# A two-layer hybrid trunk: eight heads' rows of the first output projection in full float32, and another order of its rows

## The chip, the cores and the metric

The program runs on one core of a Trainium2 chip. The time is the device time of one execution in microseconds; the kernel before is timed in three runs, and their median is used. The engines of the core work side by side, each through its own list of instructions in order: TensorE (PE in the profile, its loads of stationary operands PEld), VectorE (DVE), ScalarE (ACT), GpSimd (POOL) and SyncE (SP), which here only issues transfers.

## The reference, cut to what matters

A decoder of two layers over 256 positions of width 2048, in float32. Layer 0 mixes with a forgetting attention of 16 heads, layer 1 with a windowed attention; after each mixer comes a gated ConvFFN. A conditioning vector c gives shift, scale and gate of every sub-layer.

```python
for i in range(DEPTH):
    mod = c_act @ ada_w[i] + ada_b[i]
    sh1, sc1, g1, sh2, sc2, g2 = jnp.split(mod[:, None, :], 6, axis=-1)
    h = x * (1.0 + sc1) + sh1
    y = fox_attention(...) if i % 2 == 0 else swa_attention(...)
    x = layer_norm(DEEPNORM_ALPHA * x + (1.0 + g1) * y, ...)
    h = x * (1.0 + sc2) + sh2
    y = conv_ffn(...)
    x = layer_norm(DEEPNORM_ALPHA * x + (1.0 + g2) * y, ...)
...
def fox_attention(h, w_in, b_f, w_o):
    ...
    o = o.transpose(1, 0, 2, 3, 4).reshape(B, S, FOX_WIDTH)
    return o @ w_o
```

The place of the change is the last line: the outputs of the 16 heads, 256 x 2048, times w_o, 2048 x 2048. One head is 128 columns of o and 128 rows of w_o.

## The kernel before, in words

Large products are made in fp32r, a rounded form of float32. To keep float32's accuracy each operand is split into a high half (the rounded value) and a low half (what is left), and three products are made for one: high with high, high with low, low with high. Of the weights, `stream` (L231) loads a raw tile w, four row blocks of 128 by 512 columns (1 MB), ScalarE casts two row blocks to wh (L252), and VectorE takes the difference wl (L264). Of the heads, ScalarE casts the output o from PSUM (L84) and VectorE takes the difference (L85), into tiles oT or, for heads 12 to 15, into the store hH of the layer's input, which is no longer needed.

The output projection (`out_proj`, L765) multiplies with the heads as the stationary operand and 512 columns of weights moving. There are four column blocks d and eight pairs of heads kc in each. One pair in one column block is a unit: two halves of the sequence, two heads, three products, 12 in all. Column blocks 0 and 1 are done side by side in three stretches of rows, 0 to 7, 8 to 11 and 12 to 15; then block 2 and block 3 run through all rows. In block 3 the last four units do the first half of the sequence first, so that its LayerNorm can start (`x_mm_end`, `Edge.end`).

The heads are begun in blocks of four in the order 0, 2, 1, 3 (heads 0 to 3, 8 to 11, 4 to 7, 12 to 15) and run as generators behind the matrix products: each unit ends with `tick`, which moves every running head by a step: scores S, softmax (pr, with its sums on VectorE at L721 and L733 and its exponentials on ScalarE at L725 and L735), transposes T with their copy pT, and the product with V, o. If a unit needs a head that is not ready, `stat` steps the heads until it is. The same `tick` advances the conditioning: 0.72 columns a unit, each a 1 MB transfer wa and a reduction on VectorE (L406).

The raw tiles w, the columns wa and the rows of the LayerNorm share one pool of six buffers of 1 MB, and SyncE issues their transfers in program order, each when its buffer is free. A scheduler merges all this into one list for each engine, which then runs in that order.

Of the kernel before, what the change touches and what calls it, by code (L numbers as in the profile page):

```python
# [17 lines left out]
P = 128  # L18
# [23 lines left out]
def hybrid_trunk(ctx: ExitStack, tc: tile.TileContext, a: dict, out: bass.AP):  # L42
# [34 lines left out]
    def pin(ins, on=True):  # L77

        if on:
            tc.keep_in_program_order(ins)  # L80
# [145 lines left out]

    halves = []

    def stream(wsrc, row0, col, ks, use, spare={}):

        ks, pend = list(ks), {}  # L231
        for kc in ks[::2]:
            g = row0 + kc
            src = wsrc[g // UK, col // WB]
            if kc in pend:
                w = pend[kc]
            elif g % UK == 0 and kc + 2 in ks:
                W = wtile()
                pin(nc.sync.dma_start(W, src), False)
                w, pend[kc + 2] = W[:, :2], W[:, 2:]  # L240
            else:
                if halves:
                    w = halves.pop()
                else:
                    W = wtile()
                    w = W[:, :2]
                    halves.append(W[:, 2:])
                pin(nc.sync.dma_start(w, src[:, g % UK:g % UK + 2]), False)
            h, l = spare[kc]() if kc in spare else (hl.tile([P, 2, WB], F32R, tag=n, name=n) for n in ("wh", "wl"))
            pieces = [(h, l, w)] if not isinstance(h, Pair) else [(h[:, i, :], l[:, i, :], w[:, i, :]) for i in range(2)]  # L250
            for hp, _, wp_ in pieces:
                pin(nc.scalar.copy(hp, wp_), False)  # L252

            def go(kc=kc, h=h, l=l):
                ahead[0] -= 1
                run_post()
                use(kc, h, l)
                if feeds:
                    feeds.pop(0)()
                tick()  # L260

            def residual_(pieces=pieces, go=go):
                for hp, lp, wp_ in pieces:
                    nc.vector.tensor_tensor(lp, wp_, f32(hp), op=ALU.subtract)  # L264
# [126 lines left out]
    def tick():  # L391
        ada_tick()
        if not feeds:
            side_step()
            step()
# [360 lines left out]

    AV = ((0, 0, 2 * P), (P, 2 * P, 3 * P))

    def o_tile(kc):

        if kc >= KC - 4:
            return hH[:, kc, :], hL[:, kc, :]
        g = gtile("oT")
        return g[:, 0, :], g[:, 1, :]

    def out_proj(oT, full, w_o, l, edge):
        def stat(kc, t):
            while kc not in full:
                step()
            return oT[kc][0][:, t * P:(t + 1) * P], oT[kc][1][:, t * P:(t + 1) * P]  # L770

        ps = {d: x_banks() for d in range(2)}

        def part(d, ks):
            if d == D // WB - 1:
                stream(w_o, 0, d * WB, ks, x_mm_end(ps[d], stat, KC, HEAD, edge.end), spares(KC, HEAD, True))
            else:
                stream(w_o, 0, d * WB, ks, lambda kc, h, l_: x_mm(ps[d], kc, h, l_, stat, KC - 1))

        for i, ks in enumerate((range(0, 8), range(8, 12))):  # L780
            then(lambda i=i: ada.update(rate=(0.72, 0.43)[l]))
            for d in range(2):
                part(d, list(ks))
        then(lambda: (ada_need(l, 2), ada.update(rate=(0.72, 0.65)[l])))
        for d in range(D // WB):
            if d < 2:
                part(d, list(range(12, KC)))
            else:
                ps[d] = x_banks()
                part(d, list(range(KC)))  # L790
            if d < D // WB - 1:
                then(lambda d=d: defer(residual(ps[d], d, gates[l, 2], True)))
                then(lambda d=d: ada.update(rate=(0.72, 0.65)[l] if d < D // WB - 2 else 0.0))
        then(lambda: (flush(), ada.update(gate_free=True)))


    def fox(l, j, edge):
# [84 lines left out]
        def head(blk, hh, q, k, V):  # L882
# [22 lines left out]
            def outputs(pT):  # L905
                ops = bank("o")
                for b, (d0, s0, s1) in enumerate(AV):
                    mm(ops[:, d0:S], V[b][:, hs], pT[:, s0:s1], start=b == 0, stop=b == 1, skip_group_check=True)
                oT[h] = o_tile(h)
                full.add(h)  # L910
                split(*oT[h], ops[:, :S])

            hs = slice(hh * P, (hh + 1) * P)
            yield from attend(scores, outputs)
# [94 lines left out]
    def swa(l, j, edge, after):  # L1009
# [49 lines left out]
        def pair(g, n, q):  # L1059
# [39 lines left out]
            oT[kc] = o_tile(kc)  # L1099
            full.add(kc)  # L1100
            split(*oT[kc], ops[:, :S])

        ps = head_block(w_in, KOFF, after.start)
        then(lambda: ada.update(rate=.1))
# [163 lines left out]
```

## Time and profile before

| | us |
|---|---|
| median of three runs (2185.02 to 2186.53) | 2186.52 |
| profiled execution | 2185.4 |
| its span, first to last instruction | 2183.6 |
| output projection of layer 0, first product to the first turn of x behind it | 337.3 to 456.3 |

Mean granted clock of TensorE 0.994. A row of the timeline gives start, duration, engine, line, operation, the tile written and the tiles read, the shape, how many instructions are merged into the row, and in brackets the idle time of the engine ahead of it with what ended it. A row of groups gives total busy time, the mean of one in ns, and the idle time before them. TensorE's rows overlap: one product's end is covered by the next one's start, so the pace is read from starts.

### The profile page before, as it was taken

Reading aid. Unit: us, or ns where it says so; the run is one execution under the profiler, and the core shown is the slowest. Engines: PE = TensorE matmul, PEld = TensorE weight load, DVE = VectorE, ACT = ScalarE, POOL = GpSimd, SP = SyncE. Lnnn points to the kernel's source line nnn. Section 1 sums busy time; section 2 is a strip of 40 time slices with the busy share of each in tenths; the row PEclk is TensorE's granted clock in tenths of the full one; section 3 lists DMA queues with packets and bytes.
Section 4 is the critical chain, followed back from the end, with each engine's and each line's share of the span. In section 5 each row is a group of like instructions: output and inputs, shape, how many; then the busy total and the mean of one; then the engine's idle time right before and its main releaser. Section 6 shows DMA issues by size and latency. Waiting matters only on the chain.

```text
span 2183.6 us, 35813 instructions
## 1 busy us (share of the span) xinstructions
PE 2129.5 (98%) x14488; PEld 1932.3 (88%) x14488; DVE 1763.2 (81%) x2425; ACT 1169.7 (54%) x1805; POOL 11.8 (1%) x34
## 2 busy tenths in 40 slices
PE   6999999899999999999999999999999999999997
PEld 6999887779999888999987877779999888999986
DVE  7988899989889988898997897779788655666765
ACT  4546566445575433555555677655555633555541
POOL 1000000000000000000000000000000000000000
PEclk9999999999999999999999999999999999999999
DMA  9998988948888999887885665547777555555552
GB/s 387 421 372 302 369 332 339 348 171 337 315 301 315 336 344 362 324 329 293 326 327 231 250 251 193 172 146 297 272 270 272 199 194 195 195 195 195 193 195 99
DMA packets 89654, 598.60 MB, mean 274 GB/s; under 512 B 10016, under 2 KB 12352, under 8 KB 21136
## 3 DMA queue, kind: packets, MB, share of 16 engines
q1 hardware_dynamic: 89312, 595.87, 73.7%
q8 instruction: 113, 1.85, 0.3%
q0 software_dynamic: 176, 0.44, 0.1%
q14 instruction: 53, 0.43, 0.1%
HBM read 594.18 MB, written 2.10 MB: 273 GB/s over the span
## 4 chain that ended last, share of the span: by engine, by line
PE 82%; DVE 10%; ACT 5%; issue 1%; DMA 1%; SPq 0%; POOL 0%; DVEq 0%; ACTq 0%; POOLq 0%
PE ws L75 46%; PE xs L75 34%; DVE wa L406 3%; DVE wl L264 3%; ACT wh L252 2%; DMA w<-in_fox_w_in_dram 1%; ACT pr L725 1%; DVE pr L721 1%; PE o L75 0%; DVE x L646 0%; ACT pr L1088 0%; DVE stats L648 0%; PE T L752 0%; PE sm L75 0%; PE sm L488 0%
## 5 line engine op out<-in xcount | busy, mean ns | idle before, releaser
L252 ACT CAST wh<-w 128x1024 fp32r<-128x1024 f32 x712 | 749.1, 1055 | 748.0 <-PE xs L75 336.5
L264 DVE TENSOR_TENSOR wl<-w,wh 128x1024 fp32r<-128x1024 f32 x712 | 866.4, 1223 | 328.5 <-ACT wh L252 325.9
L75 PE MATMUL ws<-hH,wh 128*128 128x256 f32 x6400 | 1098.0, 276 | 8.0 <-ACT hH L515 7.2
L75 PEld LDWEIGHTS ws<-hH,wh 128*128 128x128 f32 x6400 | 968.3, 188 | 11.4 <-ACT hH L515 7.6
L75 PE MATMUL ws<-hH,wl 128*128 128x256 f32 x3200 | 879.9, 276 | 2.4 <-DVE wl L264 2.4
L75 PEld LDWEIGHTS ws<-hH,wl 128*128 128x128 f32 x3200 | 601.3, 188 | 3.4 <-DVE wl L264 3.4
L406 DVE CUSTOM_DVE_ANT_0 wa<-wa,cb,acol 128x2048 f32<-128x2048 f32 x192 | 450.0, 2347 | 0.2 <-DVE cb L134 0.2
L75 PE MATMUL xs<-wh,gT 128*128 128x512 f32 x1344 | 414.7, 389 | 0.0
L75 PEld LDWEIGHTS xs<-wh,gT 128*128 128x128 f32 x1344 | 252.3, 188 | 52.1
L75 PE MATMUL xs<-wh,hH 128*128 128x512 f32 x800 | 269.4, 402 | 6.2 <-ACT wh L252 2.4
L75 PE MATMUL xs<-wl,gT 128*128 128x512 f32 x672 | 261.4, 389 | 0.0
L75 PEld LDWEIGHTS xs<-wh,hH 128*128 128x128 f32 x800 | 149.3, 189 | 41.8 <-ACT hH L84 3.5
L75 PE MATMUL xs<-wl,hH 128*128 128x512 f32 x400 | 158.4, 396 | 3.3 <-DVE wl L264 3.3
L75 PEld LDWEIGHTS xs<-wl,gT 128*128 128x128 f32 x672 | 126.1, 188 | 26.3
L1123 ACT ACTIVATE u<-ws,ccol 128x256 f32<-128x256 f32 x176 | 97.0, 563 | 51.8 <-PE ws L75 42.1
L75 PE MATMUL xs<-wh,oT 128*128 128x512 f32 x352 | 119.1, 407 | 0.2 <-ACT oT L84 0.2
L1124 DVE SCALAR_TENSOR_TENSOR u<-ws,ccol,u 128x255 f32<-128x255 f32 x176 | 82.6, 479 | 14.0 <-ACT u L1123 14.0
L75 PEld LDWEIGHTS xs<-wl,hH 128*128 128x128 f32 x400 | 75.6, 189 | 18.6 <-DVE wl L264 3.9
L1126 DVE SCALAR_TENSOR_TENSOR u<-ws,ccol,u 128x254 f32<-128x254 f32 x176 | 83.8, 480 | 2.2
L75 PEld LDWEIGHTS xs<-wh,oT 128*128 128x128 f32 x352 | 68.2, 194 | 15.6 <-ACT oT L84 0.7
L75 PE MATMUL xs<-wl,oT 128*128 128x512 f32 x176 | 71.2, 405 | 6.8 <-DVE wl L264 6.8
L725 ACT ACTIVATE pr<-pr,nm 128x128 f32<-128x128 f32 x96 | 43.3, 454 | 29.9 <-DVE nm L721 29.7
(210 smaller groups left out, 1195.2 us busy)
## 6 DMA issues: line engine op xcount, KB each, us to landing
wa<-in_ada_w_dram SPq DMA_DIRECT2D x192, 1024.0 KB, 6.9
w<-in_ffn_w_up_dram SPq DMA_DIRECT2D x176, 1024.0 KB, 5.1
w<-in_ffn_w_down_dram SPq DMA_DIRECT2D x88, 1024.0 KB, 5.0
w<-in_fox_w_in_dram SPq DMA_DIRECT2D x60, 512.0 KB, 8.3
w<-in_swa_w_in_dram SPq DMA_DIRECT2D x20, 1024.0 KB, 5.6
w<-in_fox_w_in_dram SPq DMA_DIRECT2D x18, 1024.0 KB, 7.4
w<-in_fox_w_o_dram SPq DMA_DIRECT2D x16, 1024.0 KB, 6.9
w<-in_swa_w_o_dram SPq DMA_DIRECT2D x16, 1024.0 KB, 4.8
```

Source lines behind the costliest of these rows:

```text
L75: return nc.tensor.matmul(o, lhsT, rhs, start=start, stop=stop, **kw)
L252: pin(nc.scalar.copy(hp, wp_), False)
L264: nc.vector.tensor_tensor(lp, wp_, f32(hp), op=ALU.subtract)
L406: return nc.vector.tensor_tensor_reduce(w, w, cb, 1.0, acol[:, l, v * KC + k:v * KC + k + 1], ALU.mult, ALU.add, cv[:, k:k + 1])
L721: nc.vector.tensor_tensor_reduce(pr[:, b:e].rearrange("p (a k) -> p a k", k=P), S_ps[:, b:e].rearrange("p (a k) -> p a k", k=P), mk, -1.0, ...
L725: nc.scalar.activation(pr[:, b:e], pr[:, b:e], AF.Exp, bias=nm[:, r:r + 1], scale=-1.0, accum_out=ss[:, r:r + 1])
L1123: nc.scalar.activation(u, pf, AF.Identity, bias=cw(CW, f), scale=cw(2, f))
L1124: nc.vector.scalar_tensor_tensor(u[:, 1:], pf[:, :S - 1], cw(1, f), u[:, 1:], op0=ALU.mult, op1=ALU.add)
L1126: nc.vector.scalar_tensor_tensor(u[:, 2:], pf[:, :S - 2], cw(0, f), u[:, 2:], op0=ALU.mult, op1=ALU.add)
```

## The change

In layer 0, heads 4 to 7 and 12 to 15 are whole: ScalarE copies their output unrounded to a float32 tile oW (two heads to a tile), and nothing is left over for a low half. The rows of w_o that belong to them are not cast and have no residual: the raw tile w is the moving operand, and there is one float32 product where there were three. Of the 32 units of the projection 16 are whole: four of the eight pairs in each of the four column blocks. In column blocks 0 and 1 the rows come in the order 0 to 3, 8 to 11, 4 to 7, 12 to 15. The second layer's projection is as before.

```diff
-    def stream(wsrc, row0, col, ks, use, spare={}):
+    def stream(wsrc, row0, col, ks, use, spare={}, whole=()):
...
+            if kc in whole:
+                add(kc, w, None, use)
+                continue
             h, l = spare[kc]() if kc in spare else (hl.tile([P, 2, WB], F32R, tag=n, name=n) for n in ("wh", "wl"))
...
-            def residual_(pieces=pieces, go=go):
+            def split_(pieces=pieces):
                 for hp, lp, wp_ in pieces:
                     nc.vector.tensor_tensor(lp, wp_, f32(hp), op=ALU.subtract)
-                del residuals[go]
-
-            ahead[0] += 1
-            weights.add(go)
+
+            add(kc, h, l, use, split_)
+
+    def add(kc, h, l, use, split_=None):
+
+        def go():
+            ahead[0] -= 1
+            run_post()
+            use(kc, h, l)
+            if feeds:
+                feeds.pop(0)()
+            tick()
+
+        def residual_():
+            split_()
+            del residuals[go]
+
+        ahead[0] += 1
+        weights.add(go)
+        if split_:
             residuals[go] = residual_
-            work.append(go)
-            settle(2)
+        work.append(go)
+        settle(2)
 
     def x_mm(ps, kc, h, l, stat, last, first=0, ts=range(NT), js=range(2)):
 
         for t in ts:
             for i in js:
                 xh, xl = stat(kc + i, t)
+                if l is None:
+                    mm(ps[t], xh, h[:, i, :], start=kc + i == first, stop=kc + i == last)
+                    continue
                 mm(ps[t], xh, h[:, i, :], start=kc + i == first)
                 mm(ps[t], xh, l[:, i, :])
                 mm(ps[t], xl, h[:, i, :], stop=kc + i == last)
...
-    def o_tile(kc):
-
+    WHOLE = ((*range(4, 8), *range(12, KC)), ())
+
+    wide = []
+
+    def o_tile(kc, src, l):
+
+        if kc in WHOLE[l]:
+            if not wide:
+                g = f32(gtile("oW"))
+                wide.extend(g[:, i, :] for i in range(2))
+            o = wide.pop(0)
+            nc.scalar.copy(o, src)
+            return o, None
         if kc >= KC - 4:
-            return hH[:, kc, :], hL[:, kc, :]
-        g = gtile("oT")
-        return g[:, 0, :], g[:, 1, :]
+            o = hH[:, kc, :], hL[:, kc, :]
+        else:
+            g = gtile("oT")
+            o = g[:, 0, :], g[:, 1, :]
+        split(*o, src)
+        return o
...
-        for i, ks in enumerate((range(0, 8), range(8, 12))):
-            then(lambda i=i: ada.update(rate=(0.72, 0.43)[l]))
+        early, late = (range(0, 8), range(8, 12)) if l else ((*range(0, 4), *range(8, 12)), range(4, 8))
+        for ks in (early, late):
+            then(lambda: ada.update(rate=(0.72, 0.43)[l]))
             for d in range(2):
                 part(d, list(ks))
```

The lists of three engines show what moves. First TensorE, at the third stretch of rows, where the heads of block 3 end. Before, a unit with the transposes T of one of them ahead of the next unit:

```order
L752 MATMUL T<-ident,pr 128x128 x3
L75 MATMUL xs<-wh,oT 128x512
L75 MATMUL xs<-wl,oT 128x512
L75 MATMUL xs<-wh,oT 128x512 x2
L75 MATMUL xs<-wl,oT 128x512
L75 MATMUL xs<-wh,oT 128x512 x2
L75 MATMUL xs<-wl,oT 128x512
L75 MATMUL xs<-wh,oT 128x512 x2
L75 MATMUL xs<-wl,oT 128x512
L75 MATMUL xs<-wh,oT 128x512
L752 MATMUL T<-ident,pr 128x128 x3
```

Now:

```order
L75 MATMUL xs<-w,oW 128x512 x4
L766 MATMUL T<-ident,pr 128x128 x3
L75 MATMUL xs<-w,oW 128x512 x4
L766 MATMUL T<-ident,pr 128x128 x3
L75 MATMUL xs<-w,oW 128x512 x4
L75 MATMUL o<-pT,v 128x256
L75 MATMUL o<-pT,v 128x128
L766 MATMUL T<-ident,pr 128x128 x3
L75 MATMUL xs<-w,oW 128x512 x4
L75 MATMUL o<-pT,v 128x256
L75 MATMUL o<-pT,v 128x128
```

A unit of 12 products has become one of four, and the ends of the heads stand closer together, one or two whole units ahead of the rows that need them.

Second VectorE, ahead of the residuals for the fifth and sixth unit of column block 2 (t, x and stats are the LayerNorm rows of the finished column blocks 0 and 1; ISA rows are the reductions wa, each with the read of its sum). Before:

```order
L644 TENSOR_TENSOR t<-xs,gate 128x512
L648 BN_STATS stats<-x 128x6
L406 ISA wa,cv<-wa,cb,acol 128x2048
L406 ISA cv 128x1
L264 TENSOR_TENSOR wl<-w,wh 128x1024
L646 TENSOR_TENSOR x<-x,t 128x512
L264 TENSOR_TENSOR wl<-w,wh 128x1024
L648 BN_STATS stats<-x 128x6
L406 ISA wa,cv<-wa,cb,acol 128x2048
L406 ISA cv 128x1
L644 TENSOR_TENSOR t<-xs,gate 128x512
L646 TENSOR_TENSOR x<-x,t 128x512
```

These are followed by stats, one more wa and the two residuals. Now:

```order
L658 TENSOR_TENSOR t<-xs,gate 128x512 x2
L660 TENSOR_TENSOR x<-x,t 128x512 x2
L662 BN_STATS stats<-x 128x6
L420 ISA wa,cv<-wa,cb,acol 128x2048
L420 ISA cv 128x1
L662 BN_STATS stats<-x 128x6
L420 ISA wa,cv<-wa,cb,acol 128x2048
L420 ISA cv 128x1
L259 TENSOR_TENSOR wl<-w,wh 128x1024 x2
```

The residuals of the third and fourth unit, which stood among these rows, are gone; the LayerNorm rows and the columns wa have stayed.

Third SyncE's list of transfers with what each waits for, at the same place in both programs (DVE, PE and Activation are the engines whose last read frees the buffer, DMAHW an earlier transfer). Before:

```order
L405 DMA wa<-in_ada_w_dram 128x2048 [waits DMAHW2_49,DVE_49]
L239 DMA w<-in_fox_w_o_dram 128x2048 [waits DMAHW4_49,DMAHW3_49,DVE_49]
L405 DMA wa<-in_ada_w_dram 128x2048 [waits DVE_49]
L405 DMA wa<-in_ada_w_dram 128x2048 [waits DMAHW6_49,DMAHW5_49,DVE_49]
L239 DMA w<-in_fox_w_o_dram 128x2048 [waits DVE_49]
L405 DMA wa<-in_ada_w_dram 128x2048 [waits DMAHW7_49,DMAHW1_49,DVE_49]
L239 DMA w<-in_fox_w_o_dram 128x2048 [waits DMAHW0_49,DVE_49]
```

Now:

```order
L419 DMA wa<-in_ada_w_dram 128x2048 [waits DMAHW2_49,DVE_49]
L239 DMA w<-in_fox_w_o_dram 128x2048 [waits DMAHW3_49,DVE_49]
L419 DMA wa<-in_ada_w_dram 128x2048 [waits DMAHW4_49,PE_49]
L419 DMA wa<-in_ada_w_dram 128x2048 [waits DMAHW5_49,DVE_49]
L239 DMA w<-in_fox_w_o_dram 128x2048 [waits DMAHW6_49,DVE_49]
L419 DMA wa<-in_ada_w_dram 128x2048 [waits DMAHW7_49,PE_49]
L239 DMA w<-in_fox_w_o_dram 128x2048 [waits DMAHW0_49,DVE_49]
```

The sequence of the transfers is the same; two of the columns wa shown, and five in the projection, now wait for TensorE, since a raw tile of whole rows is read by TensorE itself.

More of the change, by code (lines that the diff above doesn't have):

```diff
@@ L775, in part @@
             if d == D // WB - 1:
-                stream(w_o, 0, d * WB, ks, x_mm_end(ps[d], stat, KC, HEAD, edge.end), spares(KC, HEAD, True))
+                stream(w_o, 0, d * WB, ks, x_mm_end(ps[d], stat, KC, HEAD, edge.end), spares(KC, HEAD, True), WHOLE[l])
             else:
-                stream(w_o, 0, d * WB, ks, lambda kc, h, l_: x_mm(ps[d], kc, h, l_, stat, KC - 1))
-        for i, ks in enumerate((range(0, 8), range(8, 12))):
-            then(lambda i=i: ada.update(rate=(0.72, 0.43)[l]))
+                stream(w_o, 0, d * WB, ks, lambda kc, h, l_: x_mm(ps[d], kc, h, l_, stat, KC - 1), whole=WHOLE[l])
+        early, late = (range(0, 8), range(8, 12)) if l else ((*range(0, 4), *range(8, 12)), range(4, 8))
+        for ks in (early, late):
+            then(lambda: ada.update(rate=(0.72, 0.43)[l]))
             for d in range(2):
```

15 lines of the change are left out of this document (3 added, 12 removed).

## The prediction

> **What bounds the kernel now.** First the page's top, then the output projection by stage (length, then busy time of TensorE, its weight loads, VectorE, ScalarE and GpSimd, granted clock, share of the DMA engines, GB/s).
>
> ```profile
> span 2183.6 us, 35813 instructions
> PE 2129.5 (98%) x14488; PEld 1932.3 (88%) x14488; DVE 1763.2 (81%) x2425; ACT 1169.7 (54%) x1805; POOL 11.8 (1%) x34
> ...
> 337.30:355.10 17.80, 13.40 (x57) 10.33 (x57) 15.23 (x27) 13.12 (x32) 0.00 (x0) 0.90 0.85 321
> 355.10:400.20 45.10, 45.10 (x225) 37.71 (x224) 42.65 (x64) 24.26 (x48) 0.00 (x0) 1.00 0.92 342
> 400.20:426.60 26.40, 23.86 (x97) 19.06 (x96) 23.10 (x24) 8.42 (x8) 0.00 (x0) 0.94 0.92 354
> 426.60:456.30 29.70, 25.02 (x97) 19.30 (x95) 23.87 (x32) 9.04 (x10) 0.57 (x1) 0.89 0.73 273
> sum 119.00, PE 107.38 PEld 86.39 DVE 104.85 ACT 54.84 POOL 0.57; mean PE 26.84 PEld 21.60 DVE 26.21 ACT 13.71 POOL 0.14
> ```
>
> The kernel as a whole is TensorE's; these 119.0 us are not. TensorE is idle for 119.0 - 107.38 = 11.6 us of them, and where it had been idle the granted clock falls to 0.90, 0.94 and 0.89. The timeline of TensorE shows the waits, the waits in this stretch the engine behind them:
>
> ```profile
> 338.28 0.33 PE L752 MATMUL T<-ident,pr 128*128 128x128 f32 x1 [0.86 <-ACT pr L735]
> ...
> 348.77 0.84 PE L752 MATMUL T<-ident,pr 128*128 128x128 f32 x3 [3.23 <-ACT pr L735]
> 414.29 0.50 PE L75 MATMUL xs<-wl,oT 128*128 128x512 f32 x1 [2.54 <-DVE wl L264]
> 437.27 0.80 PE L75 MATMUL xs<-wl,oT 128*128 128x512 f32 x1 [4.25 <-DVE wl L264]
> ...
> PE xs L75 <- DVE wl L264: 6.8, 2, 4.3
> ```
>
> Two waits are for wl, the low half of a weight pair, from VectorE; the 3.23 are for a head of block 1 (heads 4 to 7), asked for while it is still in its softmax. For the price of TensorE's work I read the chain of waits where TensorE ran without a gap (start, length, what):
>
> ```profile
> 364.14 0.92 PE S L75 x8
> 368.73 2.75 PE xs L75 x12
> 371.48 0.33 PE T L752 x3
> 377.67 0.65 PE o L75 x4
> ```
>
> A unit (two heads' rows of the weights against both halves of the sequence, 12 products) takes 2.75 us; of a head, the scores S take 0.92, the transposes T 0.33, the product with V (o) 0.65. The stretch holds 32 units, 4 S, 8 T and 8 o: 88.0 + 3.7 + 2.6 + 5.2 = 99.5 us. **Lost: 119.0 - 99.5 = 19.5 us**, idle and slow clock together. The 57 records up to 355.1 are 36 products (3 units), 12 of T, 8 of o and one at the edge, 10.9 us: 6.9 lost. In the last two stages (56.1 us, 16 units, 44.0 us) 12.1 are lost, in the second 0.5.
>
> **The change part by part.** *TensorE.* 16 of the 32 units become whole: four products of full float32 for twelve of fp32r. The trace has full float32 in o; two products of a head, 256 and 128 columns, are four records. By shape:
>
> ```profile
> L75 PE MATMUL ws<-hH,wh 128*128 128x256 f32 x6400 | 1098.0, 276 | 8.0 <-ACT hH L515 7.2 <-DVE hH L517 0.8
> L75 PE MATMUL o<-pT,v 128*128 128x256 f32 x32 | 9.5, 379 | 0.0
> ```
>
> 32 records for 16 heads: each such product is two records. Each lasts 103 ns longer than an fp32r record of the same shape, some 230 columns more at the unit's 2.75 us / (12 x 512) = 0.448 ns a column: it reads its columns about twice. So a full product is four passes, and one for three is more work, not less. Pace: 0.65 us for 2 x (256 + 128) = 768 record columns, 0.846 ns; a 512-column record 0.433, a product 0.867, a whole unit 3.47 us. **Added: 16 x (3.47 - 2.75) = 11.5 us**, on the engine that sets the pace. Bounds: four unoverlapped halves of 379 ns a product, 1.52 us, give 6.1 us a unit and +53 us; two records at fp32r pace, 0.46, give 1.8 and -15 us. I take the o pace, the same kind of operand in a stream, and allow 0.79 to 0.90 ns a column (3.24 to 3.67 a unit): the one from eight records of o in a row (1536 columns, 1.22 us to the next start), the other two fp32r passes of 0.448.
>
> ```profile
> 355.11 1.47 PE L75 MATMUL o<-pT,v 128*128 128x256 f32 x8
> 356.33 0.30 PE L75 MATMUL S<-Bm,A 128*128 128x128 f32 x1
> ```
>
> [...]
>
> *VectorE and ScalarE.* Groups of the 119.0 us:
>
> ```profile
> L406 DVE CUSTOM_DVE_ANT_0 wa<-wa,cb,acol 128x2048 f32<-128x2048 f32 x18 | 42.2, 2342 | 0.0
> L264 DVE TENSOR_TENSOR wl<-w,wh 128x1024 fp32r<-128x1024 f32 x32 | 38.6, 1220 | 4.1 <-ACT wh L252 4.0
> L648 DVE BATCH_NORM_STATS2 stats<-x 128x6 f32<-128x512 f32 x7 | 4.8, 689 | 0.0
> L644 DVE TENSOR_TENSOR t<-xs,gate 128x512 f32<-128x512 f32 x7 | 4.8, 688 | 8.7 <-PE xs L75 8.7
> L646 DVE TENSOR_TENSOR x<-x,t 128x512 f32<-128x512 f32 x7 | 4.8, 685 | 0.0
> ...
> 410.76 2.33 DVE L406 CUSTOM_DVE_ANT_0 wa<-wa,cb,acol 128x2048 f32<-128x2048 f32 x1
> 413.02 0.08 DVE L406 DVE_READ_ACCUMULATOR2_ANT cv<- 128x1 f32 x1
> 413.02 2.36 DVE L264 TENSOR_TENSOR wl<-w,wh 128x1024 fp32r<-128x1024 f32 x2
> ```
>
> Two wl in a row take 2.36 us, a wa 2.26. VectorE loses 16 wl (18.9 us) and 8 low halves of oT; ScalarE 16 casts. This alone is worth nothing; it pays where VectorE makes TensorE wait. In the last two stages VectorE works 23.10 + 23.87 = 47.0 us against TensorE's 44.0, and the loads of the later units stand behind conditioning columns (wa) and LayerNorm rows. After, it is 47.0 - 8 x 1.18 = 37.6 against 8 x 2.75 + 8 x 3.47 = 49.8.
>
> Does the order allow it? At the first of the two waits, column block 2 begins at 400.2 and its fifth unit got wl at 414.29, 14.1 later. Now VectorE has, from the start of the block, two t, two x, two stats (0.69 each), two wa (2.26) and one wl (1.18) ahead of that unit: 9.8 us. TensorE asks after two split and two whole units, 12.4 us. At the second, two t, a wa, two x, two stats and one product for G and B precede the first remaining residual: some 8 us, asked for after 12.4. **Both waits go: -12.1 us.**
>
> *Heads.* The first eight units are now rows 0 to 3 and 8 to 11, whose heads are done; block 1 has until about 370 (355.1, four more units, four S and one o). But the first units stand behind the same work:
>
> ```profile
> 342.57 2.35 DVE L406 CUSTOM_DVE_ANT_0 wa<-wa,cb,acol 128x2048 f32<-128x2048 f32 x1
> 345.57 1.03 ACT L252 CAST wh<-w 128x1024 fp32r<-128x1024 f32 x1
> 346.63 1.23 DVE L264 TENSOR_TENSOR wl<-w,wh 128x1024 fp32r<-128x1024 f32 x1 [0.55 <-ACT wh L252]
> 348.32 0.80 ACT L735 ACTIVATE pr<-pr,ss 128x128 f32<-128x128 f32 x2
> ```
>
> TensorE stands from 345.5 to 346.6 for wh, then 0.7 for wl, then 0.3 for pr, after the 0.9 before its first T; with an estimated 0.6 at the restarts 3.6 are lost instead of 6.9, **-3.3 us**. [...] New: where a head's o is copied just ahead of its use, TensorE waits for that copy:
>
> ```profile
> 389.53 0.37 ACT L84 CAST hH<-o 128x256 fp32r<-128x256 f32 x1
> ```
>
> Heads 12 and 13, then 14 and 15: 0.37 and the latency, 0.55 twice, **+1.1**.
>
> *Transfers.* Their number and bytes stay; what changes is how long a raw weight tile is held: until TensorE's last read, no longer until VectorE's. Six buffers serve the weights and wa, and five wa issues now wait for TensorE. Landing times of the projection's loads, and the queue's longest wait for VectorE before:
>
> ```profile
> DMA to landing us min/median/max: 4.8/6.9/8.9
> ...
> SPq L239 <- DVE wl L264: 31.3, 9, 8.2
> ```
>
> A held tile is freed at the end of its second unit. Behind the issue that waits for it stand the loads of later units, and the tightest is that for units five and six of column block 2. Bound: if the tile waited for is the one read last before that block, the load is third behind it: 6.9, twice 3.0 (1.05 MB at 354 GB/s), cast 1.05 and wl 1.18, 15.1 us against 12.4, so 2.7 late. If it is any earlier whole tile, the load has at least 6.9 us more and nothing is late. The other buffers turn over faster than the held ones, so an older tile is likelier: **0**, the bound kept for a rival.
>
> **Sum:** 11.5 - 12.1 - 3.3 + 1.1 = **-2.8 us**. The profiled execution took 2185.4 us, 1.8 outside its span, and lies 1.1 below the median of 2186.5; 2.8 off gives 2182.6 for it and **2183.7** for the median. The gain is what is left of 15.4 us of waits after 12.6 us of price.
>
> **The rivals.** (1) *Larger gain.* Full float32 runs at 0.79 ns a column and a whole unit takes 3.24 us: 3.7 less, 2180.0; if VectorE's shorter queue also clears half of the early wait, 2178.2. For it: eight records in a row ran so, and no stream of 512-column full products is in the trace. Against: the four of a head, the commoner case, took 0.846. (2) *No change.* A pass costs what an fp32r pass costs, a whole unit 3.67: +3.2, 2186.9. For it: xs runs at 0.448 ns a column where o runs at 0.423 a pass, so streams of 512 columns may be the slower ones. Against: o has weight loads of the same size and more switches. [...] (3) *Slower: held tiles starve the fifth unit.* Place: units five and six of column blocks 2 and 3. Price: 2.7 us each by the bound above, and after each a slow clock, which in the last two stages came to 12.1 - 2.54 - 4.25 = 5.3 us for two waits, so 2.7 + 2.7 twice, 10.8: 2194.5; in one block alone 2189.1. It decides from the point where wl comes more than 12.4 us after the block began. For it: DMA was at 0.92 of its time in both stages, and the queue issues in order. Against: TensorE is the slower engine there by 49.8 to 37.6, and an earlier tile leaves 6.9 us. (4) That the change does not do what it says is ruled out by the program's order: the whole units are there, the residuals gone.
>
> **How the numbers follow.** Chances: forecast 0.50, larger gain 0.22, no change 0.14, slower 0.14. 0.2% is 4.4 us, about what a measurement of this kernel can tell from no change, so the forecast itself lies within it. It spreads by the pace (0.79 to 0.90 ns, 3.7 down and 3.2 up) and by a microsecond or two of heads: of its 0.50, 0.13 are faster by more than that, 0.36 within and 0.01 slower. The larger gain is faster with all of its 0.22; of no change 0.13 are within and 0.01 faster; of slower 0.12 are slower and 0.02 within. Together **faster 0.36, same 0.51, slower 0.13**. The range runs from rival 1's lower end to a little past one starved block: **2178 to 2190.5**.
>
> **What would show it.** Right: xs from w and oW with 128 records (16 units x 4 products x 2), starting 0.43 us apart, a whole unit in 3.47; no wait of TensorE for wl over 1 us in the two last column blocks, granted clock near 1.00 there; about 3.5 us lost before the ninth unit, and waits of some 0.5 us for the copy of o; 16 wl fewer; the stage about 116 us instead of 119.0, and the stages behind it unchanged. Wrong: a record pace away from 0.433 moves the time by 1.28 us for each 0.01; a wait for wl or for a w transfer at a fifth unit is rival 3; a stage that shortens with a total that does not means that the gain is given back in the ConvFFN behind it.

## The result, and the profile after

| | before | after |
|---|---|---|
| median on the same chip, 10 runs each | 2186.11 | 2180.15 |
| profiled execution | 2185.4 | 2180.0 |
| its span | 2183.6 | 2178.1 |
| first product of the stage to the ConvFFN's first turn of x | 131.8 | 126.7 |

The ratio is 0.9978, with a 95% interval of 0.9970 to 0.9986: faster by 6.0 us by the medians, by 4.8 us (3.1 to 6.6) by the ratio. The forecast was 2183.7, a gain of 2.8 us, within a range of 2178 to 2190.5; by the medians the change gained twice that. The prediction thought it likeliest that the gain stays within 0.2%; the interval has that bound inside it. Of all executions in this document three took 3401, 4320 and 4351 us (one of vector_back, one of the kernel before, one of four_split); the ratios leave them out, and without them the medians of vector_back and four_split below are 2179.98 and 2183.79.

The last row of the table is a length that all kernels below have too. Its ends are these two rows of TensorE's timeline, first before, then after:

```profile
338.37 0.72 PE L75 MATMUL xs<-wh,oT 128*128 128x512 f32 x2
...
470.20 0.65 PE L488 MATMUL sm<-ident,x 128*128 128x128 f32 x4
```

```profile
337.98 0.72 PE L75 MATMUL xs<-wh,oT 128*128 128x512 f32 x2
...
464.68 0.66 PE L502 MATMUL sm<-ident,x 128*128 128x128 f32 x4
```

5.1 of the 5.5 us that the span lost are in this stage. The page's first line and the stage by windows, after (length, then busy time of TensorE, its weight loads, VectorE, ScalarE and GpSimd, granted clock, share of the DMA engines, GB/s):

```profile
span 2178.1 us, 35629 instructions
...
336.90:354.80 17.90, 15.43 (x74) 12.04 (x74) 14.97 (x25) 13.97 (x33) 0.00 (x0) 1.00 0.84 313
354.80:401.10 46.30, 46.30 (x178) 28.90 (x176) 33.25 (x50) 14.22 (x38) 0.00 (x0) 1.00 0.90 335
401.10:425.70 24.60, 24.60 (x81) 15.03 (x80) 21.00 (x23) 4.01 (x4) 0.00 (x0) 1.00 0.97 378
425.70:450.80 25.10, 24.51 (x80) 14.70 (x78) 15.38 (x23) 5.99 (x6) 0.57 (x1) 1.00 0.76 284
sum 113.90, PE 110.84 PEld 70.67 DVE 84.61 ACT 38.19 POOL 0.57; mean PE 27.71 PEld 17.67 DVE 21.15 ACT 9.55 POOL 0.14
```

TensorE is busier than before in the stage (110.84 against 107.38), yet the stage is 5.1 us shorter. The granted clock is 1.00 in all four windows, where it was 0.90, 0.94 and 0.89 in three. The new operation, by its tile oW, and TensorE's timeline at the places of which the prediction spoke:

```profile
L75 PE MATMUL xs<-w,oW x128: 590/592/667, 370.0 to 452.2; 128*128 128x512 f32 x128
L784 ACT COPY oW<-o x8: 350/372/373, 349.5 to 391.3; 128x256 f32<-128x256 f32 x8
```

```profile
346.27 0.73 PE L75 MATMUL xs<-wh,oT 128*128 128x512 f32 x2 [1.09 <-ACT wh L255]
347.53 0.50 PE L75 MATMUL xs<-wl,oT 128*128 128x512 f32 x1 [0.53 <-DVE wl L259]
...
370.00 3.60 PE L75 MATMUL xs<-w,oW 128*128 128x512 f32 x8
373.43 0.49 PE L766 MATMUL T<-ident,pr 128*128 128x128 f32 x3
...
406.96 7.03 PE L75 MATMUL xs<-w,oW 128*128 128x512 f32 x16
414.06 0.40 PE L75 MATMUL xs<-wl,oT 128*128 128x512 f32 x1
...
450.83 1.11 PE L539 MATMUL sm<-ident,x 128*128 128x128 f32 x8 [0.63 <-DVE x L688]
```

A whole unit, eight records, takes 373.43 - 370.00 = 3.43 us (3.44 over 17 units in a row, in whole_all below). Between 347.5 and 450.2 TensorE waits for nothing: the waits of 2.54 and 4.25 us are gone. By the prediction's count the work in the stage is now 16 x 2.75 + 16 x 3.44 + 11.5 for the heads = 110.5 us, so 113.9 - 110.5 = 3.4 us are lost, where 19.5 were.

### The profile page after: what moved, and what is told of

Same layout as the page of the kernel before. It is cut to its first block, busy times and chain, and to the rows that moved or that the text cites. A ratio compares the mean times of both kernels' runs of the same rounds, so it can differ in the third digit from the quotient of the medians.

```text
span 2178.1 us, 35629 instructions
## 1 busy us (share of the span) xinstructions
PE 2133.7 (98%) x14424; PEld 1916.9 (88%) x14424; DVE 1742.4 (80%) x2400; ACT 1151.8 (53%) x1788; POOL 11.8 (1%) x34
## 4 chain that ended last, share of the span: by engine, by line
PE 84%; DVE 9%; ACT 4%; DMA 2%; issue 1%; SPq 0%; POOL 0%; DVEq 0%; ACTq 0%; POOLq 0%
PE ws L75 46%; PE xs L75 35%; DVE wa L420 3%; DVE wl L259 2%; DMA w<-in_fox_w_in_dram 2%; ACT wh L255 1%; DVE pr L735 1%; PE o L75 1%; PE S L75 1%; ACT pr L739 0%; PE T L766 0%; ACT hH L551 0%; PE sm L75 0%; PE sm L502 0%; DVE hH L552 0%
## 5 line engine op out<-in xcount | busy, mean ns | idle before, releaser
L255 ACT CAST wh<-w 128x1024 fp32r<-128x1024 f32 x698 | 733.0, 1053 | 726.8 <-PE ws L75 340.2
L259 DVE TENSOR_TENSOR wl<-w,wh 128x1024 fp32r<-128x1024 f32 x698 | 847.8, 1221 | 328.6 <-ACT wh L255 326.1
L75 PE MATMUL xs<-wh,hH 128*128 128x512 f32 x752 | 254.0, 403 | 6.5 <-ACT wh L255 3.2
L75 PEld LDWEIGHTS xs<-wh,hH 128*128 128x128 f32 x752 | 140.3, 189 | 40.3 <-ACT wh L255 3.7
L75 PE MATMUL xs<-wl,hH 128*128 128x512 f32 x376 | 148.9, 396 | 2.5 <-DVE wl L259 2.5
L75 PE MATMUL xs<-wh,oT 128*128 128x512 f32 x288 | 96.1, 401 | 1.1 <-ACT wh L255 1.1
L75 PEld LDWEIGHTS xs<-wl,hH 128*128 128x128 f32 x376 | 71.0, 189 | 16.9 <-DVE wl L259 3.2
L75 PEld LDWEIGHTS xs<-wh,oT 128*128 128x128 f32 x288 | 53.9, 188 | 13.2 <-ACT wh L255 1.3
L658 DVE TENSOR_TENSOR t<-xs,gate 128x512 f32<-128x512 f32 x48 | 31.5, 683 | 35.0 <-PE xs L75 35.0
```

The lines of the kernel that those rows point to most:

```text
L75: return nc.tensor.matmul(o, lhsT, rhs, start=start, stop=stop, **kw)
L658: pin(nc.vector.tensor_tensor(tmp, ps[t], gate[:, d * 512:(d + 1) * 512], op=ALU.mult), end)
```

## The experiments

All times are medians of 5 to 11 runs; each kernel was timed together with the kernel before, whose medians on those chips were 2184.4 to 2185.3. "Stage" is the length defined above, from each kernel's profiled execution; in the last two kernels the work ahead of the first product lies otherwise, and the length is left out.

| kernel | time | ratio to before, 95% | stage |
|---|---|---|---|
| before | 2186.11 | | 131.8 |
| the change | 2180.15 | 0.9978 (0.9970 to 0.9986) | 126.7 |
| order_only | 2184.01 | 0.9996 (0.9987 to 1.0005) | 131.1 |
| whole_old_order | 2179.87 | 0.9978 (0.9970 to 0.9987) | 126.6 |
| whole_4to7 | 2177.05 | 0.9965 (0.9952 to 0.9977) | 124.0 |
| whole_12to15 | 2183.60 | 0.9996 (0.9987 to 1.0005) | 130.8 |
| vector_back | 2180.16 | 0.9978 (0.9968 to 0.9987) | 126.7 |
| from_vector | 2180.73 | 0.9981 (0.9972 to 0.9990) | 126.6 |
| four_split | 2183.86 | 0.9995 (0.9986 to 1.0004) | 129.9 |
| from_copy | 2179.92 | 0.9977 (0.9968 to 0.9986) | 126.8 |
| late_4to7 | 2178.21 | 0.9968 (0.9956 to 0.9980) | 124.8 |
| whole_all | 2184.95 | 0.9999 (0.9990 to 1.0007) | 133.6 |
| first_units | 2178.36 | 0.9971 (0.9960 to 0.9982) | |
| first_late | 2177.37 | 0.9968 (0.9956 to 0.9980) | |

### The two edits apart

*order_only*: nothing whole, rows in the new order.

```diff
-    WHOLE = ((*range(4, 8), *range(12, KC)), ())
+    WHOLE = ((), ())
```

> The new order of the rows (0 to 3, 8 to 11, 4 to 7, 12 to 15) with no whole rows: three products and all splits stay. Theory (two separate effects: the order clears the early wait for heads 4 to 7, the whole rows clear the two waits for wl in column blocks 2 and 3 and cost TensorE 11.0 us): the early part gains about 3.5 us, the two late waits stay, and a part of the early gain is lost there since VectorE sets the time from 394 us on: 2182.5 to 2185. Rival (the order is the whole gain and the float32 products only cost): faster than the full change, 2175 or less.

2184.01 us, within the theory's range, and no difference from the kernel before that can be told. Its timeline shows the early part cleared as in the change, and the late waits back, the first of them longer than the 2.54 of before:

```profile
346.26 0.73 PE L75 MATMUL xs<-wh,oT 128*128 128x512 f32 x2 [1.09 <-ACT wh L255]
...
412.87 0.80 PE L75 MATMUL xs<-wl,oT 128*128 128x512 f32 x1 [4.32 <-DVE wl L259]
...
436.75 0.50 PE L75 MATMUL xs<-wl,oT 128*128 128x512 f32 x1 [3.75 <-DVE wl L259]
```

Most of what the order gains early, TensorE spends in longer waits for wl: 9.3 us in blocks 2 and 3 (0.46 and 0.78 beside the two shown), where it was 6.8.

*whole_old_order*: the eight heads whole, rows 0 to 7, then 8 to 11.

```diff
-        early, late = (range(0, 8), range(8, 12)) if l else ((*range(0, 4), *range(8, 12)), range(4, 8))
+        early, late = range(0, 8), range(8, 12)
```

> Heads 4 to 7 and 12 to 15 whole as in the change, rows in the old order (0 to 7, 8 to 11). Theory: TensorE pays 11.0 us, the two late waits (12.1 us with their slow clock) go, the wait for heads 4 to 7 at 345 us stays: 2184 to 2187. Rival (the order is the whole gain): 2186.1 + 11.0, about 2197. Rival (the whole rows are the whole gain): 2180.

The rival held: the same time as the change. One early wait is left, for the copy of a head of block 1, half of the 3.23 us of before, and none up to the LayerNorm:

```profile
348.20 1.13 PE L75 MATMUL xs<-w,oW 128*128 128x512 f32 x2 [1.68 <-ACT oW L784]
```

So the order is worth nothing that can be told here, alone or beside whole rows.

### Which rows

*whole_4to7* and *whole_12to15*: only one half of the whole heads, new order.

```diff
-    WHOLE = ((*range(4, 8), *range(12, KC)), ())
+    WHOLE = ((*range(4, 8),), ())
```

```diff
-    WHOLE = ((*range(4, 8), *range(12, KC)), ())
+    WHOLE = ((*range(12, KC),), ())
```

> Only heads 4 to 7 whole, heads 12 to 15 split as before the change; the new order. Theory: the price on TensorE is half, 5.5 us; both late waits still go, since in column block 2 the fifth unit asks for its low half 12.3 us after the block began and VectorE has 9.8 us ahead of it, and in column block 3 the unit that waited 4.25 us is one of the whole ones: 2186.1 - 3.5 - 12.1 + 5.5, about 2176. Rival (relief goes by the number of whole units): midway between the order alone and the full change, 2181 to 2183.

> Only heads 12 to 15 whole, heads 4 to 7 split; the new order. Theory (it counts where in a column block the low halves are missing, not how many): the price is 5.5 us, but in column block 2 the fifth unit asks after 11.0 us with 12.2 us of VectorE's work ahead of it, a wait of 1 us or more, and the third unit of column block 3 waits as before, 4 us with a slow clock behind it: 2182 to 2185. Rival (any half of the whole rows does): as with heads 4 to 7, about 2176.

Both times came as expected. Heads 4 to 7 alone, half the price, lie 3.1 us below the change (the stage is 2.7 us shorter, though the intervals of the two ratios overlap) and have one late wait, at the first unit of block 3; heads 12 to 15 alone leave both. First the timeline of the former, then of the latter:

```profile
425.05 0.50 PE L75 MATMUL xs<-wl,oT 128*128 128x512 f32 x1 [1.45 <-DVE wl L259]
```

```profile
413.92 0.50 PE L75 MATMUL xs<-wl,oT 128*128 128x512 f32 x1 [2.41 <-DVE wl L259]
436.25 0.50 PE L75 MATMUL xs<-wl,oT 128*128 128x512 f32 x1 [4.25 <-DVE wl L259]
```

The first wait is at the fifth unit of block 2, the second at the third unit of block 3. Heads 4 to 7 are the third and fourth units of a block: just ahead of the first wait, and at the place of the second itself. Heads 12 to 15 are the seventh and eighth: behind the first wait, and two units ahead of the second.

### VectorE's relief, or TensorE's pace

The prediction laid the late waits to VectorE's load. A whole unit spares VectorE a residual, waits for nothing that VectorE makes, and keeps TensorE 0.69 us longer. Three kernels part these.

*vector_back*: VectorE gets its work back, and nobody reads it.

```diff
             if kc in whole:
-                add(kc, w, None, use)
+                idle = hl.tile([P, 2, WB], F32R, tag="wl", name="wl")
+                def idle_(w=w, idle=idle):
+                    nc.vector.tensor_tensor(idle, w, w, op=ALU.subtract)
+                add(kc, w, None, use, idle_)
```

> The change, and for each of its 16 whole units VectorE also runs an operation of the shape of a residual, whose result nothing reads (wl = w - w, 128x1024): the work of VectorE is that of before again, the work of TensorE that of the change. Theory: VectorE is relieved by 1.2 us a unit, but a whole unit needs no result of VectorE at all, and TensorE asks for the fifth unit of a column block later by 0.69 us for each whole unit ahead of it; of the 12.1 us of late waits at most some 2 to 4 come back, as waits for wl of 1 to 2 us at the first split unit behind the whole ones. 2181 to 2184 us. Rival: it is the shorter queue of VectorE alone that clears them; then both waits return with 2.5 us or more each, and with the price of 11.0 us still paid the time is 2189 or more. Second rival: the queue is worth nothing, 2180.

2180.16 us, the time of the change: the second rival. VectorE's groups and the timelines of VectorE and TensorE at the fifth unit of block 2:

```profile
L253 DVE TENSOR_TENSOR wl<-w 128x1024 fp32r<-128x1024 f32 x16 | 19.1, 1213 | 0.0
```

```profile
412.04 2.36 DVE L264 TENSOR_TENSOR wl<-w,wh 128x1024 fp32r<-128x1024 f32 x2
```

```profile
413.84 0.40 PE L75 MATMUL xs<-wl,oT 128*128 128x512 f32 x1
```

With 19.1 us of VectorE's work put back, wl is begun at 412.04 and ready at 413.2, and TensorE asks at 413.84.

*from_vector*: each whole unit also waits for VectorE, which makes a copy of the raw tile in the residual's place.

```diff
-                add(kc, w, None, use)
+                copy = f32(hl.tile([P, 2, WB], F32R, tag="wl", name="wl"))
+                def copy_(w=w, copy=copy):
+                    nc.vector.tensor_tensor(copy, w, w, op=ALU.max)
+                add(kc, copy, None, use, copy_)
```

> The change, but TensorE multiplies a whole unit from a copy of the raw weights that VectorE makes in the place of the residual (max of the tile with itself, 128x1024, the residual's duration): VectorE has its work of before back, and each whole unit also waits for VectorE as a split one does for its low half. Theory: in the run with the idle operations put back, these stood 1 to 4 us ahead of TensorE's use, so waiting for them costs little: 2180 to 2182. Rival: freedom from VectorE is what the whole units gain; then waits for these copies of over 1 us at the third and seventh units of the last column blocks or in the first half of the stage, and 2184 or more.

2180.73, as the theory had it; TensorE waits for none of the copies. Freedom from VectorE is not the gain either.

*four_split*: nothing is whole; the same 16 units get a fourth product instead.

```diff
-                mm(ps[t], xl, h[:, i, :], stop=kc + i == last)
+                mm(ps[t], xl, h[:, i, :], stop=kc + i == last and not four)
+                if four:
+                    mm(ps[t], xl, l[:, i, :], stop=kc + i == last)
```

> Order of the change, every unit split as before, and in the 16 units that the change makes whole a fourth product, low half of o by low half of the weights: 16 products at the unit's 2.75 / 12 = 0.229 us each, 3.67 us a unit. VectorE and ScalarE have all work of before, TensorE waits for wl wherever it did; only TensorE's pace is that of the change or a little slower. Theory: the waits are filled by TensorE's own extra work, since VectorE then has 1.4 us more up to each fifth unit and 14.7 us more in the stage; the waits for wl shrink to under 1 us each, the clock stays at 1.00, and the time is the change's plus 16 x (3.67 - 3.44) = 3.7 us: 2183.8, between 2183 and 2187. Rival: the waits go because the whole units need no low half; then they stay as in the run with the order alone (4.3 and 3.75 us), and the time is that run's 2184.0 plus 14.7 us: 2195 to 2199.

2183.86, the theory's 2183.8. The kernel does all the work of before and 16 x (3.63 - 2.75) = 14.1 us more on TensorE (3.63 by the rows below, two units in 7.25), and is no slower. VectorE's timeline at the fifth unit of block 2, TensorE's from the third unit on, and the windows:

```profile
412.52 1.22 DVE L259 TENSOR_TENSOR wl<-w,wh 128x1024 fp32r<-128x1024 f32 x1
```

```profile
410.72 0.39 PE L75 MATMUL xs<-wh,oT 128*128 128x512 f32 x1
...
417.97 0.62 PE L75 MATMUL xs<-wh,oT 128*128 128x512 f32 x2
418.43 0.39 PE L75 MATMUL xs<-wl,oT 128*128 128x512 f32 x1
```

```profile
400.00:425.00 25.00, 25.00 (x111) 20.50 (x110) 24.97 (x28) 8.45 (x8) 0.00 (x0) 1.00 0.80 292
425.00:450.00 25.00, 24.95 (x109) 20.02 (x109) 21.84 (x26) 10.11 (x11) 0.00 (x0) 1.00 0.98 381
```

VectorE works 24.97 of 25 us in the first window, and TensorE does not wait for it. The same two dates in five kernels, ready being the start of VectorE's row and 1.18 us, asked the start of TensorE's row without its wait:

| fifth unit of block 2 | wl ready | asked for |
|---|---|---|
| order_only | 412.8 | 408.5 |
| before | 414.2 | 411.7 |
| change | 411.1 | 414.1 |
| vector_back | 413.2 | 413.8 |
| four_split | 413.7 | 418.4 |

The rows behind order_only and the change on VectorE:

```profile
411.59 2.36 DVE L259 TENSOR_TENSOR wl<-w,wh 128x1024 fp32r<-128x1024 f32 x2
```

```profile
409.87 2.35 DVE L259 TENSOR_TENSOR wl<-w,wh 128x1024 fp32r<-128x1024 f32 x2
```

Counted from the stage's first product, which starts at 337.7 to 339.0, VectorE's date moves by 2.8 us over all of them, TensorE's by 8.9. Up to this unit VectorE sets the pace of the stage, and TensorE, slowed by whole units or by a fourth product alike, fills with work the time in which it would wait. The change lowers VectorE's date too, but it would not have had to.

The second wait, at the third unit of block 3, is another matter. VectorE's timeline there, first before, then in four_split:

```profile
425.42 0.69 DVE L644 TENSOR_TENSOR t<-xs,gate 128x512 f32<-128x512 f32 x1 [3.23 <-PE xs L75]
426.03 2.35 DVE L264 TENSOR_TENSOR wl<-w,wh 128x1024 fp32r<-128x1024 f32 x2
...
436.01 2.35 DVE L264 TENSOR_TENSOR wl<-w,wh 128x1024 fp32r<-128x1024 f32 x2
```

```profile
423.34 3.50 DVE L259 TENSOR_TENSOR wl<-w,wh 128x1024 fp32r<-128x1024 f32 x3
...
435.31 2.34 DVE L259 TENSOR_TENSOR wl<-w,wh 128x1024 fp32r<-128x1024 f32 x2
```

Before, VectorE itself stands idle for 3.23 us, until TensorE is through with its products for the row t of the LayerNorm. The residuals of block 3's first two units come behind t in its list, and that of the third unit (at 436.01) is ready 10.6 us after the block began at 426.62; TensorE asks for it after 6.4. More work for TensorE does not by itself fill such a wait: in whole_12to15 two whole units, 1.4 us of price, stand right ahead of block 3, VectorE is idle for 4.84 us, and the wait stays 4.25. In four_split the residuals of the first two units stand ahead of t (the last two of the three at 423.34), and that of the third is ready 6.1 us after the block began at 430.43, about when TensorE comes to it. The change, whole_old_order, vector_back, from_vector and from_copy have that order too; order_only, whole_12to15, whole_4to7 and late_4to7 have the order of before. So this wait goes with VectorE's work put back as well, but only together with another order of VectorE's list; that the scheduler chose it for the slower TensorE is likely and not shown, and no run has the one without the other.

### Held tiles

*from_copy*: ScalarE copies the raw tile unrounded to a buffer of wh's kind, and TensorE multiplies from that.

```diff
-                add(kc, w, None, use)
+                copy = f32(hl.tile([P, 2, WB], F32R, tag="wh", name="wh"))
+                pin(nc.scalar.copy(copy, w), False)
+                add(kc, copy, None, use)
```

> The change, but ScalarE copies each whole weight tile unrounded into a buffer of wh's kind, and TensorE multiplies from the copy: the raw tile is released by ScalarE's copy, some 10 us earlier than by TensorE's last read. VectorE as in the change, ScalarE has the 16 weight casts of before back (1.04 us each). Theory: holding the raw tiles costs nothing on the path (TensorE waits for no transfer from the ninth unit to the end of the stage), so 2180 plus or minus 1; VectorE's wait of 1.9 us for a wa transfer shrinks and nothing follows from it. Rival (the slower one of the prediction in a weak form): later transfers cost something that the rows of TensorE do not show, then 2178 or less. Second rival: the copy itself comes late, then waits for wh of 0.5 us or more at whole units and 2182 or more.

2179.92: no difference. The longer hold is there in the change; these are its waits from 354 to 450, off TensorE:

```profile
ACT wh L255 <- DMA w<-in_fox_w_o_dram: 11.3, 1, 11.3
...
DVE wa L420 <- DMA wa<-in_ada_w_dram: 1.9, 2, 1.0
```

A cast of ScalarE waits 11.3 us for its transfer, and TensorE for nothing. In from_copy neither wait is there, and the time is the same. The price of the held tiles was rightly put at 0.

### Where the price buys something

*late_4to7*: heads 4 to 7 whole in blocks 2 and 3 alone, both forms of their o kept.

```diff
-    WHOLE = ((*range(4, 8), *range(12, KC)), ())
+    WHOLE = ((*range(4, 8),), ())
...
-                stream(w_o, 0, d * WB, ks, lambda kc, h, l_: x_mm(ps[d], kc, h, l_, stat, KC - 1), whole=WHOLE[l])
+                stream(w_o, 0, d * WB, ks, lambda kc, h, l_: x_mm(ps[d], kc, h, l_, stat, KC - 1), whole=WHOLE[l] if d > 1 else ())
```

> Heads 4 to 7 whole as in the run with these alone, but only in column blocks 2 and 3, where the late waits are; in blocks 0 and 1 their units are split (both forms of these heads are kept). 4 whole units instead of 8: 4 x 0.69 = 2.75 us less price than that run's. Theory: it is the low halves just ahead of the late waits that count; the waits stay away and the time is 2177.05 - 2.75 = 2174.3, between 2173 and 2176. Rival: VectorE enters block 2 with a backlog from blocks 0 and 1 (four more residuals, 4.8 us, and eight more halves of o), and a wait for wl of 2 us or more is back in block 2; then 2177 to 2181.

The rival held, with a wait a little below its 2 us. Four units are cheaper by 2.75 us, but TensorE comes to block 2 earlier, VectorE does not, and the wait is back:

```profile
412.93 0.50 PE L75 MATMUL xs<-wl,oT 128*128 128x512 f32 x1 [1.76 <-DVE wl L259]
425.72 0.51 PE L75 MATMUL xs<-wl,oT 128*128 128x512 f32 x1 [1.45 <-DVE wl L259]
```

*whole_all*: all 16 heads whole.

```diff
-    WHOLE = ((*range(4, 8), *range(12, KC)), ())
+    WHOLE = ((*range(KC),), ())
```

> All 16 heads whole: 32 whole units, no residual, no cast and no half of o in this projection; order as in the change. Theory: relief beyond the late waits buys nothing, and each unit still costs 0.69 us on TensorE: 16 x 0.69 = 11.0 us more than the change, less what is left of its 3.4 us of lost time (about 1 to 2), so 2189 to 2191, slower than before. Rival: VectorE's relief is worth something in itself (in the conditioning columns or the stages behind), then the stage is longer by 9 to 11 us and the total by clearly less, 2185 or below.

2184.95: slower than the change, as the theory had it, but by 4.8 where it had 9 to 11. The time is just within the rival's 2185; the rival's stage is not there, for it is 6.9 longer than the change's, where both had 9 to 11. Of the 4.1 that are missing from 11.0, 2.7 are waits: in this length TensorE is idle for 3.3 us in the change (1.09 and 0.53 early, 0.63 and 1.01 at the turn behind the stage) and for 0.5 here, where the turn's products run among the last whole units. The rest stays open; the profiled execution lies 1.2 above its median. The timeline of TensorE there, then the row of its chain of waits from which the unit's 58.45 / 17 = 3.44 us come:

```profile
393.36 62.04 PE L75 MATMUL xs<-w,oW 128*128 128x512 f32 x144
455.93 0.66 PE L539 MATMUL sm<-ident,x 128*128 128x128 f32 x4 [0.53 <-DVE x L688]
456.43 1.88 PE L75 MATMUL xs<-w,oW 128*128 128x512 f32 x4
```

```profile
393.52 58.45 PE xs L75 x136
```

*first_units*, then *first_late*: beside heads 4 to 7, heads 0 and 1 whole in blocks 0 and 3, then in block 3 alone, kept in both forms.

```diff
-    WHOLE = ((*range(4, 8), *range(12, KC)), ())
+    WHOLE = ((0, 1, *range(4, 8)), ())
...
-                stream(w_o, 0, d * WB, ks, lambda kc, h, l_: x_mm(ps[d], kc, h, l_, stat, KC - 1), whole=WHOLE[l])
+                stream(w_o, 0, d * WB, ks, lambda kc, h, l_: x_mm(ps[d], kc, h, l_, stat, KC - 1), whole=WHOLE[l] if d < 1 else WHOLE[l][2:])
```

In first_late the last line ends in `whole=WHOLE[l][2:])`; block 3 has a line of its own and takes all of WHOLE in both.

> Heads 4 to 7 whole in all column blocks, and heads 0 and 1 (kept in both forms) whole in column blocks 0 and 3, at the two places where the run with heads 4 to 7 alone still waits: 1.10 for wh and 0.53 for wl at the first unit of the stage, 1.45 for wl at the first unit of block 3. Two more whole units, 2 x 0.69 = 1.4 us, against 3.1 us of waits: 2177.05 - 1.7 = 2175.3 if the waits go for good; 2177 to 2178.5 if each only moves one unit on.

> As the run with two more whole units, but heads 0 and 1 (still kept in both forms) are whole in column block 3 only; the first unit of the stage is split again. One more whole unit than with heads 4 to 7 alone. Theory: that run lost its gain to a wait of 5.65 us some 70 us ahead of the stage, which came from the first unit of the stage being whole (its place in the buffers and the order moved the work around it); without that the earlier wait is gone, the wait of 1.45 at block 3 stays away, and the time is 2177.05 - 1.45 + 0.69 = 2176.3. Rival: the second form of o for heads 0 and 1 moves the earlier work; then the wait of 5.65 is still there and the time is 2178 or more.

Neither beats whole_4to7; first_units lies within its second range, but not for the reason given there. In first_units TensorE does not wait from 343.5 to the LayerNorm's turn at 450, but it waits at a place 70 us ahead of it, for a gate of the conditioning, and so it does in first_late, timelines in this order:

```profile
271.81 0.80 PE L75 MATMUL sm<-dh,onesr 128*128 128x512 f32 x1 [5.65 <-ACT dh L457]
```

```profile
269.53 0.79 PE L75 MATMUL sm<-dh,onesr 128*128 128x512 f32 x1 [5.65 <-ACT dh L457]
```

The rival of first_late held for the wait: it comes with the second form of o for two early heads, which both kernels have, and not with the first unit. Its time, 2177.37, is between the two figures and not to be told from whole_4to7. The best kernel measured is whole_4to7, 2177.05 us.

## Why the prediction was right or wrong

**TensorE's price, +11.5: right.** The step from o's records to 0.433 us a record and 3.47 us a unit measured 3.44, so 16 x (3.44 - 2.75) = 11.0. Rival 1's 3.24 and rival 2's 3.67 are both out, though the time is that of rival 1. The four passes of a full product are the prediction's estimate from the records of o. four_split makes four fp32r products where a whole unit makes one of float32, and two of its units take 417.97 - 410.72 = 7.25 us, 3.63 each: the 3.44 of a whole unit come to 5% less.

**Late waits, -12.1: right in size, wrong in its reason.** Both waits went, and the slow clock with them: 0.94 and 0.89 became 1.00. The dates were near too: 9.8 us of VectorE's work ahead of the fifth unit's wl, and wl was ready 411.1 - 401.1 = 10.0 after the block began; TensorE asked after some 13. But the step said of VectorE's lost residuals that this "pays where VectorE makes TensorE wait", and set 37.6 against 49.8. With VectorE's work back at 101.8 us in the stage (vector_back; 84.6 in the change, 104.9 before) the time is the same. At the first wait it is the other side of that comparison, 49.8 against 44.0, that clears it: the price itself. At the second, the relief is not needed either, but a changed order of VectorE's list came with the price, and the two are not parted. So price and gain were not two terms: four_split paid 14.1 us on TensorE and lost nothing.

**Heads, -3.3: right in size, put down to the wrong edit.** Before the ninth unit 17.90 - 15.43 = 2.5 us of idle time are left, for wh, wl and pr as listed. No run shows the 0.6 that the step estimates at the restarts: in the whole stage 3.4 us are lost, and 113.90 - 110.84 = 3.1 of them are idle time. But the order alone hands this gain to the late wait (2.54 became 4.32), and whole rows reach the same time without it. The sum has no slow clock for the waits that are left, and in the change there was none; whole_12to15 has a clock of 0.54 behind the same waits, and before, a wait of 2.54 us had one of 0.68 behind it: this was in part luck.

**The copies of o, +1.1: wrong.** TensorE does not wait for them; only its weight loads do, 0.6 us in two waits, behind products that are still running. Nor does a run show the latency, some 0.18 us, in each 0.55: the copy at 391.30 takes 0.37, and the load that waited for it begins at 391.72, 0.05 later. **Transfers, 0: right**, and rival 3 with its starved fifth unit did not come. (The DMA share of 0.92 that it gives for both its blocks is block 2's; the stage of block 3 had 0.73.)

**The 3.2 us that were missed** (2.8 forecast, 6.0 measured): 1.1 for the copies, 0.5 for the price, 0.7 less lost time in the stage (3.4 us, where 3.6 + 0.5 were left beside the copies), 0.4 ahead of the stage, whose first product starts at 337.98 instead of 338.37, and 0.5 between the profiled executions (5.4 apart) and the medians (6.0). No one term failed; several small ones lay on the same side, and the copies are the largest. With the gain known to within 3.1 to 6.6 us, parts of half a microsecond are no more than bookkeeping.

## What to carry to other kernels

Where two engines wait for each other in turn, work added to the one that waits is free up to what its waits cost, as 14.1 us were in four_split beside 19.5 lost before, as long as the other goes on working meanwhile; where that one stands waiting in turn, as VectorE does ahead of block 3, look at the order of its list. Before a gain is put down to relief of the other engine, put the relieved work back and see. Place such work at the wait or just ahead of it, and no more of it than the wait: eight heads whole gave some 6 us, the four of them that stand there 8, all sixteen none. And where a slow clock stands behind a wait, count it as part of its price: before, it was, by the estimate below, 4.0 us beside 6.8 us of waits.

## What the runs showed that I had not expected

Several microseconds of low clock stood behind some of the long waits and not behind others: 2.54 us before had them, 2.41 us in whole_12to15 had not. Before, the windows behind the waits of 2.54 and 4.25 us:

```profile
415.00:420.00 5.00, 5.00 (x17) 3.99 (x16) 5.00 (x6) 1.05 (x1) 0.00 (x0) 0.68 0.99 418
435.00:440.00 5.00, 2.73 (x7) 2.15 (x7) 5.00 (x9) 0.22 (x1) 0.00 (x0) 0.52 0.80 236
440.00:445.00 5.00, 5.00 (x19) 4.03 (x18) 5.00 (x6) 1.21 (x2) 0.00 (x0) 0.79 0.95 400
```

Busy time times what was missing of the clock, an estimate from these rows, is 5.00 x 0.32 + 2.73 x 0.48 + 5.00 x 0.21 = 4.0 us, beside 6.8 us of waits. Behind the wait of 2.41 us in whole_12to15 the clock is 1.00, and behind that of 1.76 us in late_4to7 too, windows in this order:

```profile
415.00:420.00 5.00, 5.00 (x22) 3.81 (x21) 4.55 (x5) 2.00 (x2) 0.00 (x0) 1.00 0.96 365
```

```profile
415.00:420.00 5.00, 5.00 (x24) 4.08 (x23) 5.00 (x5) 2.11 (x2) 0.00 (x0) 1.00 1.02 431
```

Yet whole_12to15 and the change have the same early waits and differ behind them. First whole_12to15, waits and then clock, and last the change, whose waits of 1.09 and 0.53 are shown above:

```profile
345.84 0.73 PE L75 MATMUL xs<-wh,oT 128*128 128x512 f32 x2 [1.08 <-ACT wh L255]
347.10 0.50 PE L75 MATMUL xs<-wl,oT 128*128 128x512 f32 x1 [0.52 <-DVE wl L259]
```

```profile
348.00:350.00 2.00, 2.00 (x8) 1.61 (x7) 1.90 (x4) 1.58 (x7) 0.00 (x0) 0.54 1.19 426
```

```profile
348.00:350.00 2.00, 2.00 (x12) 1.60 (x11) 1.96 (x5) 2.00 (x9) 0.00 (x0) 1.00 1.00 414
```

The same 1.6 us in two pieces were followed by 0.54 in the one and by 1.00 in the other; what decides between the two kernels is not shown. And a second copy of two heads' output, 0.37 us of ScalarE each, came with a wait of 5.65 us 70 us ahead of the stage in which it is used: with an order made by a scheduler, a small tile can cost where nobody looks for it.
